# Where a half's products are split: moving the split of the previous block pair in front of the gate's convolution

## The chip, the cores and the metric

The kernel runs on one core of a Trainium2 chip. The metric is the device time of one execution in microseconds (us). Engines are named as in the profile: PE (TensorE matmuls), PEld (its weight loads), DVE (VectorE), ACT (ScalarE), POOL (GpSimd), SP (SyncE, which issues the weight DMAs).

## The reference

The program is a two-layer encoder on 256 positions of width 2048. Layer 0 mixes tokens with grouped-query attention, layer 1 with dilated sliding-window attention; each layer ends with a gated MLP, which the change is about. Cut to that:

```python
def conv_ffn(h, w_up, conv_w, conv_b, w_down):
    u = h @ w_up                                   # 2048 -> 2 * 5632
    u = depthwise_conv(u, conv_w) + conv_b         # width 3 along positions
    gate, val = jnp.split(u, 2, axis=-1)
    return (jax.nn.silu(gate) * val) @ w_down      # 5632 -> 2048
# h = h + conv_ffn(rms_norm(h, ffn_norm[i]), ...), for i in 0, 1
```

## The kernel before

**Products of three.** All is float32. A matmul operand is split into a high part rounded to the fast format (`wh`, `xh`, by ACT) and a low part, the rest (`wl`, by DVE); a product is three matmuls, of high with high, low with high and high with low. So every weight tile of 128 x 1024 costs one ACT rounding (L144, in a fast unit L179) and one DVE subtraction (L145, L180) before TensorE may use it. There are four buffers each of `wh` and `wl`, so DVE can be four tiles ahead of TensorE at most.

**The up-projection** (`ffn`, L492 on) runs in 11 pairs of column blocks of 512: pair p has gate block p and value block 11 + p. The pairs are worked in two halves, 0 to 5 and 6 to 10, and after each half the down-projection consumes its products. A usual block is four calls of `feed`, one for each 512 rows of weights, of 24 matmuls each. Pairs 2, 4, 6 and 8 (`UP`) go through `up_pair`: three feeds for the gate and three for the value, with a "fast unit" in between that does one quarter of both blocks with seven products in place of eight (a Strassen-Winograd step). The unit costs DVE four sums of weights (L178) and seven splits (L180), and a "fold" behind it (L695 to L704) brings its seven results together in a tile with the tag `st`.

**After a gate or value block** its accumulators are evacuated to `stg` by ACT (`evac_scaled`, L489), turned with positions along the free axis by two DVE transposes (L377) and 16 small copies into `u` (`turned`, L562, by POOL; at the end of a half every second one by ACT, L564), convolved by `conv` (4 ACT instructions L541, 8 on DVE, L549) into `cg` for a gate and `cv` for a value. The gate gets its silu (L588). Then `product` multiplies `cg` into `cv` (L578), and `act_split` splits the product into the operands of the down-projection. For blocks 1 and 2 of a half that is `combined`: four subtractions into a tile with the tag `st` (L617), then roundings on ACT (L320) and rests on DVE (L321); for the others it is plain, four roundings (L606) and four rests (L607). `cg`, `cv` and `st` have one buffer each.

**What sets the order.** This work is written as generators that are advanced in small steps between the matmuls. `feed` gives four steps: two advance the list `beside`, two the first generator of the queue `pending`. `up_pair`'s fast unit gives none. `gate_gen(p)` evacuates and turns gate p, waits some steps and then does value p - 1's convolution and product; in an `UP` pair it runs in `beside`, else it queues in `pending`; when `pending` is empty, in layer 0 the generator in `spare` (the bias lines of the next mixer, four small matmuls and a DMA issued by POOL) gets the step. `value_gen(p)` evacuates and turns value p, waits (4 steps after an `UP` pair, 2 after another, 5 after pair 0), does gate p's convolution, its silu, and at last `act_split` of pair p - 1. `flush` does the last value of a half. The generators yield between parts:

```python
for _ in range(4 if gate[0] in UP else 2 if last else 5):
    yield
yield from conv(gate)
yield
nc.scalar.activation(gate[2], gate[2], AF.Silu)
```

The order on each engine is then chosen by a planner, which issues what is ready in its own estimate, the earliest written first; weight splits are treated as if written 60 instructions earlier. An instruction marked `keep_in_program_order` is issued behind all that was written before it on its engine: the convolution's ACT instructions, the roundings of both splits, and the rests of `combined`. Each engine works through its queue strictly in order.

**Sums for the fast units.** `sums` (L651) prepares the operands of `up_pair`: it adds the parts of the normalised input (L655, into `cg`), makes four differences (L663, into `cv`) and splits them (L320, L321). For half 0 it runs beside pair 0, for half 1 in the first steps of pair 6. In the first half the down-projection calls `pair` twice, for output blocks 0, 1 and 2, 3; each call has two fast units of its own, whose sums use the tiles `u`.

Of the kernel before, what the change touches and what calls it, by code (L numbers as in the profile page):

```python
# [8 lines left out]
F32 = mybir.dt.float32  # L9
F32R = mybir.dt.float32r  # L10
AF = mybir.ActivationFunctionType
# [3 lines left out]
P = 128  # L15
D = 2048
NT = 256
NKT = D // P
EPS = 1e-6
NPAIR = 11  # L20
NROW = 32 * NPAIR
HALVES = ((0, 6), (6, 11))
# [3 lines left out]
UP = 2, 4, 6, 8  # L26
# [7 lines left out]
def tile_encoder(ctx: ExitStack, tc: tile.TileContext, x, xT, w_a, w_ao, q_gain, k_gain, w_b, w_bo,  # L34
                 rel_bias, gains, w_up, conv, w_down, final_norm, rope, ident_c, onehot, out):
    nc = tc.nc
# [23 lines left out]
    def nm(s):  # L60
        uid[0] += 1
        return f"{s}_{uid[0]}"
# [15 lines left out]
    def start(gen):  # L78
        if next(gen, StopIteration) is not StopIteration:
            pending.append(gen)  # L80
# [238 lines left out]
    def split_in_order(hi, lo, src):  # L319
        tc.keep_in_program_order(nc.scalar.activation(hi, src, AF.Copy))  # L320
        tc.keep_in_program_order(nc.vector.tensor_tensor(lo, src, hi.bitcast(F32), ALU.subtract))  # L321
# [32 lines left out]
    def pair_slot(kt, shape, dt=F32, name="pr"):  # L354
        return hpool.tile(shape, dt, tag=f"a{kt // 2}", name=nm(name))
# [136 lines left out]
    def ffn(l, hT, ss_in, cw, g_next, last, side=None):  # L492
        with tc.tile_pool(name=nm("fpool"), bufs=1) as fp:
# [41 lines left out]
            def halves(v):  # L535
                return v.rearrange("p (m t) -> p m t", m=2)

            def conv(blk):
                n, u, c = blk
                for j in range(4):  # L540
                    tc.keep_in_program_order(nc.scalar.activation(  # L541
                        halves(c[:, j]), u[:, j, :, :P], AF.Identity, bias=tap(n, j, 3), scale=tap(n, j, 1)))
                    if j == 1:
                        yield
                flat = u.rearrange("p j m t -> p j (m t)")
                for j in range(4):
                    cj = halves(c[:, j])
                    for i, o in ((0, 0), (2, 1)):
                        nc.vector.scalar_tensor_tensor(cj, halves(flat[:, j, o:o + NT])[:, ::-1], tap(n, j, i), cj,  # L549
                                                       ALU.mult, ALU.add)  # L550
                    if j == 1:
                        yield

            def turned(s, u, by_act=False):
                quad = quad_tile(fp, "quad", 2)
                for m in range(2):
                    quad_T(quad, slice(m, 8, 2), s[:, m])
                for i, (q, c) in enumerate(QC):
                    o = u[32 * c:32 * c + 32, :, :, 32 * q:32 * q + 32]
                    src = quad[32 * q:32 * q + 32, c].rearrange("p (j m) t -> p j m t", m=2)  # L560
                    if i % 2 == 0 or not by_act:
                        nc.gpsimd.tensor_copy(o, src)  # L562
                    else:
                        nc.scalar.activation(o, src, AF.Copy)  # L564

            def gate_gen(accs, blk, value):
                s = evac_scaled(fp, accs, rstd, 1)
                yield
                turned(s, blk[1])
                if value is not None:  # L570
                    for _ in range(4 if blk[0] in UP else 2 if blk[0] == 1 else 1):
                        yield
                    yield from product(value)
# [6 lines left out]
            def value_gen(accs, blk, gate, last):  # L580
                s = evac_scaled(fp, accs, rstd, 1)
                yield
                turned(s, blk[1], blk[0] - NPAIR in (HALVES[0][1] - 1, NPAIR - 1))
                for _ in range(4 if gate[0] in UP else 2 if last else 5):
                    yield
                yield from conv(gate)
                yield
                nc.scalar.activation(gate[2], gate[2], AF.Silu)  # L588
                if last is not None:
                    yield  # L590
                    yield from act_split(last)

            def act_split(value):
                slots, k0 = value[4:]
                cv = value[2]
                if k0 // 4 in fast:
                    slots[-1 - k0 // 4], *parts = combined(cv, k0)
                    if hf == 1:
                        plain_too(k0, 20 + 2 * fast.index(k0 // 4), *parts)
                    ready.add(k0 // 4)  # L600
                    yield
                    return
                slots.update(new_slots(range(k0, k0 + 4)))
                for j in range(4):
                    hi, lo = slots[k0 + j]
                    tc.keep_in_program_order(nc.scalar.activation(hi, cv[:, j, :], AF.Copy))  # L606
                    nc.vector.tensor_tensor(lo, cv[:, j, :], hi.bitcast(F32), ALU.subtract)  # L607
                    if j == 1:
                        yield
                ready.add(k0 // 4)  # L610
# [38 lines left out]
            picks = {}  # L649

            def sums(kg, at, r, st):  # L651
                hts = [hT[4 * kg + j][:2] for j in range(4)]
                for j, (hi, lo) in enumerate(hts):
                    with tc.issue_after(newest[0].ins):
                        nc.vector.tensor_tensor(r[:, j], hi.bitcast(F32), lo.bitcast(F32), ALU.add)  # L655
                    if j == 1:
                        yield
                v = r.rearrange("p (b j) (m t) -> p b j m t", b=2, m=2)
                st = st.rearrange("p i (j t) -> p i j t", j=2)
                a11, a21, a12, a22 = v[:, 0, :, 0], v[:, 0, :, 1], v[:, 1, :, 0], v[:, 1, :, 1]  # L660
                yield
                for o, x, y in ((0, a21, a22), (2, a21, a11), (1, a11, st[:, 0]), (3, a12, st[:, 1])):
                    nc.vector.tensor_tensor(st[:, o], x, y, ALU.subtract)  # L663
                yield
                own = [pair_slot(at + 2 * i, [P, 4, 2, P], F32R, "s") for i in range(2)]
                split_in_order(*own, st)
                pick = {q: tuple(tuple(hts[b + j][i][:, m * P:(m + 1) * P] for j in range(2)) for i in range(2))
                        for q, b, m in ((1, 0, 0), (2, 2, 0), (4, 2, 1))}
                for q, i in ((5, 0), (6, 1), (7, 2), (3, 3)):
                    pick[q] = own[0][:, i], own[1][:, i]  # L670
                picks[kg] = pick
# [37 lines left out]
            for hf, (p0, p1) in enumerate(HALVES):  # L709
# [5 lines left out]
                for p in range(p0, p1):  # L715
                    k0 = 4 * (p - p0)
                    cg = fp.tile([P, 4, NT], F32, tag="cg", name=nm("cg"))
                    cv = fp.tile([P, 4, NT], F32, tag="cv", name=nm("cv"))
                    gate, value = (p, next_u(), cg), (NPAIR + p, next_u(), cv, cg, slots, k0)

                    def gate_done(accs, gate=gate, last_value=last_value):
                        gen = gate_gen(accs, gate, last_value)
                        if gate[0] in UP:
                            next(gen)
                            beside.append(gen)
                        else:
                            start(gen)

                    first = partial(sums, 0, 16, cg, cv)
                    if p == p0 and hf == 1:  # L730
                        start(first())
                    if p == 0:
                        va = project2(w_up[l], 0, NPAIR, hT, kgs, 1, gate_done, None, (), [first])
                    elif p in UP:
                        va = up_pair(p, UP_ORDER, gate_done)
                    else:
                        gate_done(project(w_up[l], p, hT, kgs))
                        va = project(w_up[l], NPAIR + p, hT, kgs)
                    extra[0] = fp, ["raw2"]
                    start(value_gen(va, value, gate, last_value))  # L740
                    last_value = value
                    if p == 1 and side is not None:
                        spare.append(side())
# [83 lines left out]
                f0, f1 = ([(kg, None)] for kg in fast)  # L827
                if hf == 0:
                    for ns in (0, 1), (2, 3):
                        pair(wd, ns, slots, both[0] + both[3] + [(4, 0)] + f0 + [(4, 1), (5, 0)] + f1 + [(5, 1)], spot, folds,  # L830
                             None, 3 * (ns[0] == 0), ready)
                    continue
# [596 lines left out]

    hT, ss, cw = mixer_a()  # L1430
    hT, ss = ffn(0, hT, ss, cw, 2, False, bias_lines)
    hT, ss, cw = mixer_b(hT, ss)
    ffn(1, hT, ss, cw, None, True)


# [82 lines left out]
```

## Time and profile before

| | us |
|---|---|
| median of 3 runs | 2240.97 (2240.86 to 2243.26) |
| the profiled execution | 2243.49 |
| its span | 2241.7 |
| PE busy in it | 2219.9 |
| DVE busy | 1879.4 |
| ACT busy | 1344.0 |
| POOL busy | 763.5 |

Times in the trace are us from the start of the span. A matmul is listed with a duration of about 0.39 us, but the next one starts before it ends, so PE looks busy all the time; where TensorE waits a little is seen better in the number of matmuls that start in a stretch. In layer 0 the pairs of the first half run from about 257 to 518, the down-projection from 518 to 649, the second half from 649; in layer 1 the first half ends at about 1781 and the second begins at about 1911.

### The profile page before, as it was taken

The numbers are of one execution on the slowest core, as the hardware profiler recorded it, in microseconds if no ns is written. First come the engines' busy times: TensorE is split into PE (matmuls) and PEld (weight loads), VectorE is DVE, ScalarE is ACT, GpSimd is POOL, SyncE is SP. The second block draws the span as 40 slices with busy tenths as digits, with TensorE's granted clock in tenths as the row PEclk, the third lists the DMA queues.
The fourth block names the chain that finished last, engine by engine and source line by source line (L and its number), as shares of the span: only waits on it lengthen the run. The fifth ranks groups of instructions, "written<-read, shape, count | busy, mean of one in ns | idle before, by whom it ended". The sixth has DMA issues, their size and how long they took to land.

```text
span 2241.7 us, 28897 instructions
## 1 busy us (share of the span) xinstructions
PE 2219.9 (99%) x9957; PEld 1835.3 (82%) x9957; DVE 1879.4 (84%) x2385; ACT 1344.0 (60%) x1894; POOL 763.5 (34%) x1017
## 2 busy tenths in 40 slices
PE   9999999999999999999999999999999999999998
PEld 7888888887888878888888888888888878888887
DVE  6877678998898998968886878588899998989887
ACT  7676656566455666665454556566565755556664
POOL 2343255843006462040053006003746500264611
PEclk9999999999999999999999999999999999999999
DMA  8565655555656555565556555556556555556654
GB/s 302 192 216 187 217 190 190 185 198 179 206 177 226 187 198 196 199 188 195 186 185 201 175 195 171 201 184 216 179 197 213 173 190 204 208 168 208 223 198 141
DMA packets 126180, 439.59 MB, mean 196 GB/s; under 512 B 14408, under 2 KB 18248, under 8 KB 126032
## 3 DMA queue, kind: packets, MB, share of 16 engines
q1 hardware_dynamic: 123056, 429.05, 56.9%
q0 software_dynamic: 2688, 8.39, 1.5%
q8 instruction: 78, 1.28, 0.2%
q14 instruction: 70, 0.57, 0.1%
q10 hardware_dynamic: 288, 0.30, 0.0%
HBM read 432.34 MB, written 5.34 MB: 195 GB/s over the span
## 4 chain that ended last, share of the span: by engine, by line
PE 43%; DVE 9%; issue 2%; POOL 1%; DMA 1%; ACT 1%; DVEq 0%; POOLq 0%; ACTq 0%
PE acc L133 13%; PE acc L134 12%; PE acc L132 12%; DVE wl L145 3%; DVE wl L180 1%; DVE cv L549 1%; PE ps L187 1%; PE ps L188 1%; PE ps L186 1%; POOL u L562 1%; PE acc L187 1%; PE acc L188 1%; DVE cg L549 1%; PE acc L186 1%; DMA raw<-in_w_b_dram 0%
## 5 line engine op out<-in xcount | busy, mean ns | idle before, releaser
L145 DVE TENSOR_TENSOR wl<-raw,wh 128x1024 fp32r<-128x1024 f32 (+1 forms) x716 | 899.1, 1264 | 226.9 <-ACT wh L144 221.1
L144 ACT ACTIVATE wh<-raw 128x1024 fp32r<-128x1024 f32 (+1 forms) x716 | 746.1, 1048 | 519.2 <-PE acc L134 407.0
L133 PE MATMUL acc<-wl,xh 128*128 128x512 f32 x2048 | 799.3, 390 | 4.2 <-DVE wl L145 4.1
L132 PE MATMUL acc<-wh,xh 128*128 128x512 f32 x2048 | 799.1, 390 | 0.3 <-ACT wh L144 0.3
L134 PE MATMUL acc<-wh,xh 128*128 128x512 f32 x2048 | 797.1, 389 | 0.0
L562 POOL COPY u<-quad 32x256 f32<-32x256 f32 x672 | 518.5, 772 | 444.2 <-DVE quad L377 394.9
L133 PEld LDWEIGHTS acc<-wl,xh 128*128 128x128 f32 x2048 | 384.7, 188 | 88.2 <-DVE wl L145 10.1
L132 PEld LDWEIGHTS acc<-wh,xh 128*128 128x128 f32 x2048 | 384.7, 188 | 79.9 <-ACT wh L144 0.7
L134 PEld LDWEIGHTS acc<-wh,xh 128*128 128x128 f32 x2048 | 384.6, 188 | 79.4
L133 PE MATMUL acc<-wl,a 128*128 128x512 f32 x720 | 280.7, 390 | 1.1 <-DVE wl L145 0.9
L132 PE MATMUL acc<-wh,a 128*128 128x512 f32 x720 | 280.9, 390 | 0.0
L134 PE MATMUL acc<-wh,a 128*128 128x512 f32 x720 | 280.1, 389 | 0.0
L179 ACT ACTIVATE wh<-raw 128x1024 fp32r<-128x1024 f32 x112 | 118.3, 1060 | 106.5 <-PE acc L134 76.4
L133 PEld LDWEIGHTS acc<-wl,a 128*128 128x128 f32 x720 | 135.2, 188 | 30.0 <-DVE wl L145 2.8
L134 PEld LDWEIGHTS acc<-wh,a 128*128 128x128 f32 x720 | 135.1, 188 | 28.2 <-DVE a L328 0.2
L132 PEld LDWEIGHTS acc<-wh,a 128*128 128x128 f32 x720 | 135.2, 188 | 27.8
L381 POOL COPY wide<-quad 32x256 f32<-32x256 f32 x133 | 89.8, 675 | 169.3 <-DVE quad L377 159.8
L180 DVE TENSOR_TENSOR wl<-raw,wh 128x1024 fp32r<-128x1024 f32 x112 | 135.6, 1228 | 5.8 <-ACT wh L179 4.4
L398 POOL COPY wide<-quad 32x256 f32<-32x256 f32 x88 | 53.3, 605 | 234.8 <-DVE quad L377 167.8
L489 ACT ACTIVATE stg<-acc,rstd 128x512 f32<-128x512 f32 x122 | 81.2, 681 | 21.4 <-PE acc L134 13.3
L549 DVE SCALAR_TENSOR_TENSOR cg<-u,cw,cg 128x256 f32<-128x256 f32 x176 | 90.8, 560 | 1.9 <-ACT cg L541 1.9
L549 DVE SCALAR_TENSOR_TENSOR cv<-u,cw,cv 128x256 f32<-128x256 f32 x176 | 86.9, 540 | 0.0
(309 smaller groups left out, 2202.4 us busy)
## 6 DMA issues: line engine op xcount, KB each, us to landing
raw<-in_w_up_dram SPq DMA_DIRECT2D x352, 512.0 KB, 4.6
raw<-in_w_down_dram SPq DMA_DIRECT2D x176, 512.0 KB, 4.5
raw<-in_w_b_dram SPq DMA_DIRECT2D x144, 512.0 KB, 4.1
raw<-in_w_bo_dram SPq DMA_DIRECT2D x48, 512.0 KB, 4.0
raw<-in_w_a_dram SPq DMA_DIRECT2D x40, 512.0 KB, 4.8
raw<-in_w_ao_dram SPq DMA_DIRECT2D x32, 512.0 KB, 4.7
raw<-in_w_a_dram SPq DMA_DIRECT2D x16, 256.0 KB, 5.7
there<-quad POOLq DMA_DIRECT2D x6, 512.0 KB, 4.3
```

The lines of the kernel that those rows point to most:

```text
L132: nc.tensor.matmul(accs[m], xh, wh[:, j, :], start=st, stop=False)
L133: nc.tensor.matmul(accs[m], xh, wl[:, j, :], start=False, stop=False)
L134: nc.tensor.matmul(accs[m], xl, wh[:, j, :], start=False, stop=sp)
L144: nc.scalar.activation(wh[:, c], r[:, c], AF.Copy)
L145: newest[0] = nc.vector.tensor_tensor(wl[:, c], r[:, c], wh[:, c].bitcast(F32), ALU.subtract)
L179: nc.scalar.activation(wh, r, AF.Copy)
L180: nc.vector.tensor_tensor(wl, r, wh.bitcast(F32), ALU.subtract)
L381: nc.gpsimd.tensor_copy(o[32 * c:32 * c + 32, :, 32 * q:32 * q + 32], quad[32 * q:32 * q + 32, c])
L398: nc.gpsimd.tensor_copy(dst, src)
L489: nc.scalar.activation(o[:, m, :], accs[m], AF.Copy, scale=rstd[:, m:m + 1])
L549: nc.vector.scalar_tensor_tensor(cj, halves(flat[:, j, o:o + NT])[:, ::-1], tap(n, j, i), cj, ALU.mult, ALU.add)
L562: nc.gpsimd.tensor_copy(o, src)
```

## The change

In `value_gen`, except at the end of a half, the split of the previous pair's product now comes one step after the value is turned, in front of the gate's convolution; the steps that it takes are deducted from the waiting steps, with at least one wait left. The gate's silu is no longer there: it is written in the next pair's `gate_gen`, behind the turning of that gate and in front of the value's convolution and product. At the end of a half (gates 5 and 10) the order is convolution, silu, split, as before, with one waiting step ahead of the convolution in place of two and no step between the convolution and the silu. Third, `sums` is cut in two: `sums_begun` (additions and differences) is started for half 1 in the second call of the down-projection of half 0, after four waiting steps, in tiles of its own with the tags `cg` and `cv`; `sums_made` (the split) is written at the start of pair 6.

```diff
@@ gate_gen
                 turned(s, blk[1])
                 if value is not None:
+                    nc.scalar.activation(value[3], value[3], AF.Silu)
                     for _ in range(4 if blk[0] in UP else 2 if blk[0] == 1 else 1):
                         yield
                     yield from product(value)
@@ value_gen
-                turned(s, blk[1], blk[0] - NPAIR in (HALVES[0][1] - 1, NPAIR - 1))
-                for _ in range(4 if gate[0] in UP else 2 if last else 5):
+                if gate[0] + 1 in (p for _, p in HALVES):
+                    turned(s, blk[1], True)
+                    yield
+                    yield from conv(gate)
+                    nc.scalar.activation(gate[2], gate[2], AF.Silu)
+                    yield
+                    yield from act_split(last)
+                    return
+                turned(s, blk[1])
+                wait = 4 if gate[0] in UP else 5 if last is None else 2
+                if last is not None:
+                    yield
+                    for _ in act_split(last):
+                        yield
+                        wait -= 1
+                    wait -= 1
+                for _ in range(max(wait, 1)):
                     yield
                 yield from conv(gate)
-                yield
-                nc.scalar.activation(gate[2], gate[2], AF.Silu)
-                if last is not None:
-                    yield
-                    yield from act_split(last)
@@ sums
             def sums(kg, at, r, st):
+                yield from sums_begun(kg, r, st)
+                sums_made(kg, at, st)
+
+            def sums_begun(kg, r, st, wait=0):
+                for _ in range(wait):
+                    yield
                 hts = [hT[4 * kg + j][:2] for j in range(4)]
...
                     nc.vector.tensor_tensor(st[:, o], x, y, ALU.subtract)
                 yield
+
+            def sums_made(kg, at, st):
+                hts = [hT[4 * kg + j][:2] for j in range(4)]
                 own = [pair_slot(at + 2 * i, [P, 4, 2, P], F32R, "s") for i in range(2)]
-                split_in_order(*own, st)
+                split_in_order(*own, st.rearrange("p i (j t) -> p i j t", j=2))
@@ the loop over pairs
                     if p == p0 and hf == 1:
-                        start(first())
+                        sums_made(0, 16, early[1])
@@ the down-projection of half 0
                     for ns in (0, 1), (2, 3):
+                        if ns[0] == 2:
+                            early = [fp.tile([P, 4, NT], F32, tag=t, name=nm(t)) for t in ("cg", "cv")]
+                            start(sums_begun(0, *early, 4))
                         pair(wd, ns, slots, both[0] + both[3] + [(4, 0)] + f0 + [(4, 1), (5, 0)] + f1 + [(5, 1)], spot, folds,
                              None, 3 * (ns[0] == 0), ready)
```

## The prediction

> **What bounds the kernel now.** I read the shares of the engines first, then the windows (busy time and count of instructions in equal stretches), then the stretch with the longest loss, in order of time. The columns of a window are its bounds and length, then busy us and (x) instructions for PE, PEld, DVE, ACT and POOL, the granted clock, the DMA share and GB/s.
>
> ```profile
> PE 2219.9 (99%) x9957; PEld 1835.3 (82%) x9957; DVE 1879.4 (84%) x2385; ACT 1344.0 (60%) x1894; POOL 763.5 (34%) x1017
> 480.00:520.00 40.00, 40.00 (x178) 33.14 (x177) 39.06 (x54) 25.44 (x40) 25.61 (x32) 1.00 0.53 183
> 520.00:560.00 40.00, 37.03 (x153) 29.14 (x152) 34.31 (x45) 27.32 (x41) 4.24 (x8) 0.96 0.52 172
> 1742.00:1782.00 40.00, 40.00 (x179) 33.10 (x177) 39.06 (x53) 25.44 (x38) 25.61 (x32) 1.00 0.55 180
> 1782.00:1822.00 40.00, 37.40 (x154) 29.47 (x153) 34.75 (x47) 27.83 (x42) 4.23 (x8) 0.96 0.51 176
> 400.00:420.00 20.00, 20.00 (x90) 16.49 (x89) 19.96 (x29) 14.28 (x19) 14.27 (x20) 1.00 0.53 176
> 420.00:440.00 20.00, 19.34 (x86) 15.67 (x85) 18.60 (x22) 10.71 (x14) 15.46 (x19) 1.00 0.64 220
> 660.00:680.00 20.00, 19.65 (x86) 15.67 (x85) 19.97 (x20) 12.07 (x13) 0.00 (x0) 1.00 0.41 131
> 800.00:820.00 20.00, 19.29 (x83) 14.88 (x82) 19.97 (x27) 12.38 (x16) 12.47 (x16) 1.00 0.50 175
> 1676.00:1696.00 20.00, 19.82 (x88) 16.05 (x87) 18.56 (x23) 13.14 (x18) 13.92 (x16) 1.00 0.65 221
> 1926.00:1946.00 20.00, 19.95 (x88) 15.92 (x87) 19.71 (x22) 12.22 (x14) 0.00 (x0) 1.00 0.52 184
> 2065.00:2085.00 20.00, 19.80 (x87) 15.81 (x86) 19.96 (x26) 12.95 (x18) 12.47 (x16) 1.00 0.57 192
> ```
>
> TensorE is the bound, and no matmul is added or removed. A window in which nothing stops it holds 178 matmuls in 40 us, so one takes 40/178 = 0.2247 us. What can be won is the matmuls missing from other windows. At the end of the first half 178 - 153 = 25 are missing, or 5.6 us, in each of the two layers (179 - 154 again gives 25): 11.2 us. In windows of 20 us with 90 due, pair 3 (420) misses 4, the start of pair 6 (660) 4 and pair 9 (800) 7; layer 1 misses 2, 2 and 3 at the same places. That is 22, or 4.9 us. Everything this change can win is therefore near 16 us, 0.7%; it can lose more.
>
> Now the end of the half. Lines are start, duration, engine, operation, and in brackets the idle time before it with its releaser; those of ACT come first, then POOL's and DVE's; the last three are groups of the window 474 to 484, with busy us and mean ns.
>
> ```profile
> 479.07 1.06 ACT L320 ACTIVATE s<-st 128x1024 fp32r<-128x1024 f32 x1 [0.27 <-DVE st L617]
> ...
> 482.93 2.08 ACT L541 ACTIVATE cv<-u,cw 128x256 f32<-128x256 f32 x4 [1.02 <-DVE sx L321]
> ...
> 491.62 2.08 ACT L541 ACTIVATE cg<-u,cw 128x256 f32<-128x256 f32 x4 [1.99 <-DVE cv L578]
> ...
> 499.17 1.06 ACT L588 ACTIVATE cg<-cg 128x1024 f32<-128x1024 f32 x1 [2.34 <-DVE cg L549]
> 500.14 1.25 ACT L489 ACTIVATE stg<-acc,rstd 128x512 f32<-128x512 f32 x2
> ...
> 517.88 2.08 ACT L541 ACTIVATE cg<-u,cw 128x256 f32<-128x256 f32 x4 [3.76 <-POOL u L562]
> 519.87 1.05 ACT L144 ACTIVATE wh<-raw 128x1024 fp32r<-128x1024 f32 x1
> ...
> 502.96 14.89 POOL L562 COPY u<-quad 32x256 f32<-32x256 f32 x16 [6.87 <-DVE quad L377]
> ...
> 470.63 1.26 DVE L145 TENSOR_TENSOR wl<-raw,wh 128x1024 fp32r<-128x1024 f32 x1 [1.44 <-ACT wh L144]
> ...
> 475.14 0.69 DVE L704 TENSOR_TENSOR acc<-acc,fold 128x512 f32<-128x512 f32 x1
> 475.86 0.96 DVE L617 TENSOR_TENSOR st<-cv 128x256 f32<-128x256 f32 x2
> ...
> L617 DVE TENSOR_TENSOR st<-cv,st 128x256 f32<-128x256 f32 x2 | 1.0, 512 | 0.0
> L321 DVE TENSOR_TENSOR s<-st,s 128x1024 fp32r<-128x1024 f32 x1 | 1.2, 1208 | 0.0
> L321 DVE TENSOR_TENSOR sx<-cv,sx 128x512 fp32r<-128x512 f32 (+1 forms) x2 | 1.0, 544 | 0.0
> ```
>
> Read it as one chain. The split of pair 2's product begins at 475.86, right behind the last addition of pair 4's fold (L704): both use the one buffer `st`. The convolution of value 3 waits for that split (it writes `cv`, which the split reads), the convolution of gate 4 waits for product 3 (L578; it writes `cg`), the silu for that convolution, and the evacuation of gate 5 stands behind the silu at 500.14. So POOL gets gate 5 only at 502.96 and ends at 517.85, and ACT, whose convolution of gate 5 is queued by then, stands 3.76 us with the next rounding of weights (519.87) behind it. TensorE's lead over its split weights is gone from there on, while DVE had been idle before 470.63.
>
> **The change part by part.**
>
> *Split in front of the gate's convolution, pair 4.* Nothing is added; four subtractions and the roundings (1.0 + 1.0 + 1.2 + 1.0 = 4.2 us of DVE, by the rows above) move from 476 into pair 4's first three feeds, some 430 to 440, before the fold takes `st`. Value 3's convolution no longer waits for the fold, so product 3, gate 4's convolution and its silu all come earlier, and the evacuation of gate 5 loses the 2.34 us and the 1.06 us of silu ahead of it: 3.4 us. With POOL's 14.89 us unchanged, gate 5's convolution then begins at 517.88 - 3.4 = 514.5; more than the idle 3.76 us ACT cannot win. The end of the half loses 5.6 us, of which a part is clock:
>
> ```profile
> 549.80:553.20 3.40, 1.52 (x7) 0.97 (x6) 3.37 (x4) 1.06 (x1) 0.00 (x0) 1.00 0.25 82
> 553.20:556.60 3.40, 3.40 (x10) 2.63 (x9) 3.40 (x4) 1.06 (x1) 0.00 (x0) 0.50 0.79 249
> 556.60:560.00 3.40, 3.40 (x16) 2.77 (x16) 2.21 (x3) 2.46 (x3) 0.00 (x0) 1.00 0.38 147
> ```
>
> After the stretch with 7 matmuls the clock is 0.50 for 3.4 us, in which 10 run in place of 16: 6 x 0.2247 = 1.3 us. The pure wait is 5.6 - 1.3 = 4.3 us. Taking 3.4 us out leaves 0.9 us of wait and, as the stretch is then nearly full, no slow clock: I take 4.7 us per layer, 9.4 us; ends 0 (gate 5 comes no earlier) and 11.2. The Trainium skill, "TensorE: Matmul & The Clock Gate", section "What's actually happening", gives a window of 3413 ns and half rate after an idle one; the length agrees with the 3.4 us here, but the stretch before still held 7 matmuls, so a fully idle window isn't needed. By the page's rule no stall under 3.4 us would cost clock, and the rival below would be 1.3 us cheaper per place.
>
> *What it costs at pair 4.* The fast unit that follows draws on the lead:
>
> ```profile
> 431.19 1.23 DVE L145 TENSOR_TENSOR wl<-raw,wh 128x1024 fp32r<-128x1024 f32 x1 [1.37 <-ACT wh L144]
> 442.21 1.23 DVE L180 TENSOR_TENSOR wl<-raw,wh 128x1024 fp32r<-128x1024 f32 x1 [0.74 <-ACT wh L179]
> L180 DVE TENSOR_TENSOR wl<-raw,wh 128x1024 fp32r<-128x1024 f32 x7 | 8.5, 1244 | 0.9 <-ACT wh L179 0.7
> L178 DVE TENSOR_TENSOR raw<-raw,raw 128x1024 f32<-128x1024 f32 x4 | 5.2, 1302 | 0.1
> 451.39 4.62 DVE L180 TENSOR_TENSOR wl<-raw,wh 128x1024 fp32r<-128x1024 f32 x4
> 453.24 0.39 PE L187 MATMUL ps<-wl,s 128*128 128x512 f32 x1
> L607 DVE TENSOR_TENSOR a<-cv,a 128x256 fp32r<-128x256 f32 x4 | 2.3, 612 | 0.0
> ```
>
> The unit needs 8.5 + 5.2 = 13.7 us of DVE for 42 matmuls, 9.4 us. Its tightest weights end at about 451.39 + 1.2 = 452.6 and are used at 453.24: 0.6 us spare, plus idle 1.37 and 0.74 us before, together 2.7 us. Moving 4.2 us in there leaves a stall of 1.5 us. Above: the gate's convolution also steps back by one step (12 matmuls, 2.7 us), which gives 4.2 us, and the slow clock 1.3 more, 5.5. Below: 0, if the lead has room for the rest. I take 1.5, since the idle rows stand right there: 3.0 us in two layers.
>
> *Pairs 2 and 8.* Their splits are plain (2.3 us, L607) and move into DVE time with full lead, but the gate's convolution steps back by 2.7 us; their units hold the same instructions as pair 4's, so 0.6 + 0.74 us are free and the stall is between 0 and 1.4 us. I take 0.7 at four places, the middle, as neither end has a nearer row: 2.8 us.
>
> *Pairs 3 and 9.* The 2.3 us of plain splits leave the work just ahead of them. The losses there are 4, 7, 2 and 3 matmuls, 0.9, 1.6, 0.4 and 0.7 us, all under 2.3: 3.6 us won; end 0 if the queue only reorders.
>
> *Sums for pair 6.* Their additions and subtractions move into the down-projection's second call:
>
> ```profile
> L655 DVE TENSOR_TENSOR cg<-xh 128x256 f32<-128x256 f32 x4 | 1.7, 414 | 0.0
> L663 DVE TENSOR_TENSOR cv<-cg 128x256 f32<-128x256 f32 x2 | 0.8, 416 | 0.0
> L663 DVE TENSOR_TENSOR cv<-cg,cv 128x256 f32<-128x256 f32 x2 | 0.8, 416 | 0.0
> L145 DVE TENSOR_TENSOR wl<-raw,wh 128x1024 fp32r<-128x1024 f32 x5 | 6.1, 1224 | 4.6 <-ACT wh L144 4.5
> ```
>
> These groups, 3.3 us in all, leave the window 640 to 680; the last row is the group of 590 to 606, where DVE idles 4.6 us waiting for ACT and the sums can hide (without that cover they cost their 3.3 us). The loss at pair 6 is 4 and 2 matmuls, 1.3 us: won; end 0.
>
> *Silu in front of the product, halves' ends.* The silu (1.06 us) is the same instruction, ready when its convolution ends; ACT is 60% busy, and I price it at nothing; it would cost its 1.06 us at ACT's head if a rounding waited behind. At the halves' ends the convolution, silu and split only come one or two steps sooner, behind the same POOL copies: nothing. SP's queue is as before. On POOL's, the small DMA of the bias lines in `spare` comes a few steps earlier in pairs 2 and 3, as `pending` empties sooner; only the next mixer waits for it: nothing.
>
> Sum: -9.4 - 3.6 - 1.3 + 3.0 + 2.8 = -8.5 us. The profiled execution took 2243.49 us (span 2241.7); it would be 2235.0. It lies 2.5 us above the median of the runs, 2240.97, and I put the forecast against the median: 2232.5 us, -0.38%.
>
> **The rivals.** *Half's end unrelieved:* gate 5 still reaches POOL at 503, since the queue's order is a planner's and another wait takes the place of the silu. For it: the order is not written out; against: each link of the chain is shown. Then -3.6 - 1.3 + 5.8 = +0.9 us, 2241.9.
>
> *The fast units eat the gain:* all high ends, 2 x 5.5 + 4 x 1.4 = 16.6 us against 14.3 won: +2.3, 2243.3. For it: only 0.6 us spare; against: DVE has 2.1 us idle just ahead.
>
> *Slower: ACT blocked by early splits.* The rounding in the split is queued on ACT in program order; put ahead of the gate's convolution it can reach the head before DVE's subtractions are done, and the weights' roundings stand behind it, as they did for 3.76 us at 517.88. Places: pairs 3, 4, 9 and 10 of both layers, 8. At 3.76 us each it costs 30 us, less 14.3: +15.8, 2256.8; it decides from (14.3 + 4.5)/8 = 2.4 us a place. For it: DVE is full at 400 to 420 (19.96 of 20 us), so its data are late there; against: ACT waited for the split's subtractions only 0.27 us at 479.07.
>
> **How the numbers follow.** About 0.2%, 4.5 us, is what a measurement of this kernel can tell from no change. Forecast 0.71; unrelieved 0.08 and eaten 0.07 (both within 0.2%); blocked 0.14. The likeliest case has its own range 2225 (all 16 us won, no new stall) to 2236. To leave out no more than 2 in 10 the range goes up past the two middle cases, to 2244: 2225 to 2244. Faster 0.71, same 0.15, slower 0.14.
>
> **What would show it.** Right: st<-cv of pair 2 near 425 to 436 and no longer behind L704; gate 5's convolution on ACT near 514 with little idle; 520 to 560 with some 174 matmuls at clock 1.00; 660 to 680 with 90. Wrong: 440 to 460 missing over 10 matmuls or at a lower clock; POOL's copies of gate 5 still ending near 518; ACT idle for some us before L320 or L606.

## The result, and the profile after

The changed kernel takes 2241.70 us (median of 12 runs, 2240.00 to 2244.87); the kernel before, run on the same chip, takes 2243.59 us (2240.86 to 2245.51). The ratio is 0.9994 with a 95% interval of 0.9985 to 1.0003: no difference that can be told. The profiled execution after took 2244.87 us, with a span of 2243.1 (before: 2243.49 and 2241.7).

The forecast was a gain of 8.5 us. That nothing is left of it does not mean that nothing happened. These are windows of the changed kernel's trace, in the same columns as those shown of before (bounds, length, then busy us and instructions of PE, PEld, DVE, ACT and POOL, clock, DMA share, GB/s), behind the line of the engines' shares:

```profile
PE 2218.4 (99%) x9957; PEld 1833.9 (82%) x9957; DVE 1885.2 (84%) x2385; ACT 1344.4 (60%) x1894; POOL 762.8 (34%) x1017
520.00:560.00 40.00, 40.00 (x178) 33.11 (x177) 37.05 (x50) 30.39 (x46) 4.71 (x9) 1.00 0.59 181
1782.00:1822.00 40.00, 39.73 (x176) 32.59 (x175) 37.77 (x49) 30.79 (x46) 4.39 (x8) 1.00 0.55 180
660.00:680.00 20.00, 20.00 (x90) 16.54 (x90) 18.09 (x18) 12.30 (x13) 0.00 (x0) 1.00 0.52 178
400.00:420.00 20.00, 17.32 (x75) 13.82 (x74) 17.96 (x25) 14.24 (x22) 10.75 (x16) 1.00 0.51 158
440.00:460.00 20.00, 19.13 (x85) 15.53 (x84) 19.86 (x22) 11.67 (x14) 13.37 (x16) 1.00 0.35 107
780.00:800.00 20.00, 18.20 (x80) 14.42 (x79) 20.00 (x26) 11.14 (x16) 14.98 (x20) 1.00 0.46 151
1660.00:1680.00 20.00, 19.30 (x85) 15.67 (x84) 19.45 (x29) 11.47 (x17) 11.15 (x16) 1.00 0.57 181
2045.00:2065.00 20.00, 18.16 (x79) 14.73 (x80) 19.76 (x26) 11.25 (x17) 12.64 (x17) 1.00 0.55 167
```

The end of the half is full: 178 and 176 matmuls at clock 1.00, where 153 and 154 stood. So is the start of pair 6 (660 to 680: 90). In exchange, pair 3 lost 15 of the 90 matmuls due in 400 to 420, where before had all 90, and pair 9 lost 10 and 11 (780 to 800 and 2045 to 2065).

To put a price on each place I compared the start of the same-numbered matmul in both traces at the bounds of the pairs (TensorE runs the same 9957 matmuls in both; a few stand in another order inside pairs 2 and 6). The step of that difference, in us, is what each stretch lost (+) or won (-):

| stretch | forecast, both layers | layer 0 | layer 1 |
|---|---|---|---|
| pairs 2 and 8 | +2.8 | -0.33, +0.17 | +0.15, +0.28 |
| pair 3 | in the next row | +2.20 | +1.22 |
| pair 9 (forecast: pairs 3 and 9) | -3.6 | +1.35 | +2.45 |
| pair 4 | +3.0 | +1.17 | +1.49 |
| end of the half | -9.4 | -5.28 | -3.97 (+0.83 later in the down-projection) |
| sums, pair 6 | -1.3 | -0.80 | -0.54 |
| all the rest (mixers) | 0 | +1.64 | -0.66 |

The last row is from the mixers, which the change does not touch. In the first one the changed kernel has a stretch at half clock, but that is not what the 1.6 us are: four kernels of the experiments lose 1.3 to 2.2 us between the same matmuls (140 to 180) without a slow stretch, so it looks like scatter between traces. The sum is +1.4 us, which is the difference of the spans. Without the mixers it is +0.4: everything that was won at the ends of the halves and at pair 6 (9.25 - 0.83 + 1.34 = 9.8 us) was paid out again in pairs 3, 9 and 4 (7.2 + 2.7).

**Where it was won.** The chain at the end of the first half, as far as it shows in ACT's and POOL's timelines and, in the last line, DVE's (the lines of the file have moved: L628 is the L617 of before, L723 and L724 are L703 and L704):

```profile
431.85 1.04 ACT L320 ACTIVATE s<-st 128x1024 fp32r<-128x1024 f32 x1
...
502.14 1.25 ACT L489 ACTIVATE stg<-acc,rstd 128x512 f32<-128x512 f32 x2
...
520.35 2.08 ACT L541 ACTIVATE cg<-u,cw 128x256 f32<-128x256 f32 x4 [1.56 <-POOL u L562]
...
505.62 14.69 POOL L562 COPY u<-quad 32x256 f32<-32x256 f32 x16 [7.69 <-DVE quad L377]
...
427.89 1.15 DVE L628 TENSOR_TENSOR st<-cv,st 128x256 f32<-128x256 f32 x2
```

Pair 2's split now has the last two of its subtractions at 427.89 and its rounding at 431.85, ahead of pair 4's fold. TensorE is 4.67 us later by then, so on the scale of before the evacuation of gate 5 is at 502.14 - 4.67 = 497.5 (before 500.14) and its convolution at 515.7 (before 517.88, forecast 514.5), and ACT waits 1.56 us for POOL instead of 3.76. That is 2.2 us earlier; with the 1.3 us of slow clock that are gone it makes 3.5 of the 5.28 us.

A second thing changed at this place. The edit at the halves' ends, which the prediction priced at nothing, brings the first two roundings of a plain split ahead of the silu of gate 5. ACT of the kernel before comes first, then that of the changed one:

```profile
528.24 1.04 ACT L588 ACTIVATE cg<-cg 128x1024 f32<-128x1024 f32 x1
...
530.14 1.32 ACT L606 ACTIVATE a<-cv 128x256 fp32r<-128x256 f32 x4
```

```profile
523.28 0.71 ACT L617 ACTIVATE a<-cv 128x256 fp32r<-128x256 f32 x2
...
530.71 1.04 ACT L588 ACTIVATE cg<-cg 128x1024 f32<-128x1024 f32 x1
```

Every kernel below whose half's end is full has this edit as well, so its share of the gain was not separated from that of the chain.

**Where it was lost.** Pair 9 of the first layer, first DVE, then the lines of ACT that feed it:

```profile
792.21 1.41 DVE L145 TENSOR_TENSOR wl<-raw,wh 128x1024 fp32r<-128x1024 f32 x1
793.55 1.41 DVE L321 TENSOR_TENSOR s<-st,s 128x1024 fp32r<-128x1024 f32 x1
794.88 1.42 DVE L321 TENSOR_TENSOR sx<-cv,sx 128x512 fp32r<-128x512 f32 x2
796.22 0.61 DVE L321 TENSOR_TENSOR c<-cv,c 128x256 fp32r<-128x256 f32 x1
796.76 1.42 DVE L145 TENSOR_TENSOR wl<-raw,wh 128x1024 fp32r<-128x1024 f32 x1
...
790.71 1.06 ACT L320 ACTIVATE s<-st 128x1024 fp32r<-128x1024 f32 x1 [3.30 <-DVE st L628]
...
792.81 2.94 ACT L144 ACTIVATE wh<-raw 128x1024 fp32r<-128x1024 f32 x3
```

Two things are to be seen here, and they are two theories. ACT stands 3.30 us in front of the split's rounding, and three roundings of weights come behind it in one piece: the prediction's rival of the blocked ACT. And DVE does all four rests of the split in a row between two rests of weights, which begin 796.76 - 792.21 = 4.55 us apart, while TensorE uses one up in 12 matmuls, 2.7 us. TensorE stops at 798 for 1.5 us, until the second of them is done.

In pair 3 of the first layer both come together, with POOL as a third. ACT's lines stand first, then DVE's:

```profile
399.40 1.10 ACT L541 ACTIVATE cg<-u,cw 128x256 f32<-128x256 f32 x2 [4.29 <-POOL u L562]
400.41 1.04 ACT L144 ACTIVATE wh<-raw 128x1024 fp32r<-128x1024 f32 x1
...
403.37 1.06 ACT L320 ACTIVATE s<-st 128x1024 fp32r<-128x1024 f32 x1 [0.94 <-DVE st L628]
...
401.48 1.33 DVE L145 TENSOR_TENSOR wl<-raw,wh 128x1024 fp32r<-128x1024 f32 x1 [1.84 <-ACT wh L144]
402.73 0.61 DVE L628 TENSOR_TENSOR st<-cv,st 128x256 f32<-128x256 f32 x1
403.26 1.68 DVE L549 SCALAR_TENSOR_TENSOR cg<-u,cw,cg 128x256 f32<-128x256 f32 x3
404.87 1.41 DVE L321 TENSOR_TENSOR s<-st,s 128x1024 fp32r<-128x1024 f32 x1
406.21 1.41 DVE L321 TENSOR_TENSOR sx<-cv,sx 128x512 fp32r<-128x512 f32 x2
407.54 2.75 DVE L145 TENSOR_TENSOR wl<-raw,wh 128x1024 fp32r<-128x1024 f32 x2
```

The gate's convolution waits 4.29 us for POOL's copies with a rounding of weights behind it; DVE idles 1.84 us for that rounding and then does 4.8 us of other work in one piece (402.73 to 407.54). TensorE loses 3.1 us at 406 to 409; the step in the table is smaller, since before lost 0.9 us in the same pair.

### The profile page after: what moved, and what is told of

The parts are those of the page before. It is cut to its first block, busy times and chain, and to the rows that moved or that the text cites. A ratio compares the mean times of both kernels' runs of the same rounds, so it can differ in the third digit from the quotient of the medians.

```text
span 2243.1 us, 28885 instructions
## 1 busy us (share of the span) xinstructions
PE 2218.4 (99%) x9957; PEld 1833.9 (82%) x9957; DVE 1885.2 (84%) x2385; ACT 1344.4 (60%) x1894; POOL 762.8 (34%) x1017
## 4 chain that ended last, share of the span: by engine, by line
PE 42%; DVE 8%; issue 2%; DMA 2%; POOL 1%; ACT 1%; DVEq 0%; POOLq 0%; ACTq 0%
PE acc L133 12%; PE acc L132 12%; PE acc L134 12%; DVE wl L145 3%; DVE wl L180 1%; DVE cv L549 1%; PE ps L187 1%; PE ps L188 1%; PE ps L186 1%; DMA raw<-in_w_b_dram 1%; POOL u L562 1%; DMA raw<-in_w_up_dram 1%; ACT wh L144 1%; DMA raw<-in_w_down_dram 1%; DVE cg L549 1%
```

## The experiments

All times are medians on the chip; each ratio is to the kernel before on the same chip, with its 95% interval. The steps by stretch are worked out as in the table above. `FRONT` names the gates whose convolution has the split in front of it (gate 2 is convolved in pair 3, gate 3 in pair 4, gate 8 in pair 9). Where a line is named by its number, the experiments' kernels have it somewhat further down: the subtractions into st are L628 to L637, the split's roundings and rests L320, L321, L640 and L645.

A step comes from one trace of each kernel, and some places scatter. In pair 9 three kernels below keep the old split, with the same instructions in the same order on DVE, ACT and POOL as in the kernel before; their steps are -0.15, -0.20 and -0.87 in the first layer and +1.19, +0.34 and +1.31 in the second. So a step of pair 9 in the second layer says little below 1.3 us.

### One part alone: the split of pair 4

The changed kernel, with the old order for every gate that is not in `FRONT`:

```
+FRONT = (3,)
...
-                    nc.scalar.activation(value[3], value[3], AF.Silu)
+                    if value[0] - NPAIR in FRONT:
+                        nc.scalar.activation(value[3], value[3], AF.Silu)
...
+                if gate[0] not in FRONT:
+                    turned(s, blk[1])
+                    for _ in range(4 if gate[0] in UP else 2 if last else 5):
+                        yield
+                    yield from conv(gate)
+                    yield
+                    nc.scalar.activation(gate[2], gate[2], AF.Silu)
+                    if last is not None:
+                        yield
+                        yield from act_split(last)
+                    return
```

> The kernel before with the split in front of the gate's convolution (and the silu in front of the product) in pair 4 alone; the halves' ends and the sums for pair 6 as in the changed kernel; pairs 1 to 3 and 7 to 10 in the old order. Theory 'blocked' (the roundings of the early splits in pairs 3 and 9 stand on ACT for data of DVE and hold the roundings of the weights back, which gave the gain back): all other steps stay as measured in the changed kernel, half's ends -5.3 and -4.0 (then +0.8), pair 4 +1.2 and +1.5, sums -0.8 and -0.5, and pairs 3 and 9 are those of the kernel before: -7.1 us, ratio 0.9968. Rival 'whole shift' (the half's end is only relieved when every split before it is early too): the half's ends stay as before, pair 4 costs its 2.7 us, sums -1.3: +1.4 us, ratio 1.0006.

Measured: 2235.37 us, ratio 0.9960 (0.9947 to 0.9972). The steps: pair 3 +0.22 and -0.12, pair 4 +1.42 and +1.43, end of the half -5.52 and -5.40, pair 6 -0.80 and -0.54, pair 9 -0.15 and +1.19. Its windows (before had 153 and 154 matmuls in the two ends of the halves):

```profile
516.00:556.00 40.00, 40.00 (x178) 33.11 (x178) 37.44 (x49) 29.84 (x44) 4.41 (x8) 1.00 0.61 185
1774.00:1814.00 40.00, 40.00 (x178) 33.13 (x177) 37.47 (x49) 29.84 (x44) 4.41 (x8) 1.00 0.58 187
400.00:420.00 20.00, 20.00 (x90) 16.48 (x89) 19.97 (x28) 13.87 (x19) 14.33 (x19) 1.00 0.55 176
440.00:460.00 20.00, 18.88 (x83) 15.31 (x83) 19.86 (x20) 12.64 (x13) 10.11 (x12) 1.00 0.36 114
```

The one early split that the half's end needs is pair 4's; the rival that it takes the whole shift falls. Here ACT's convolution of gate 5 begins at 515.18, which is 514.0 on the scale of before (TensorE is 1.17 us later) and near the forecast 514.5. It comes 3.9 us earlier, and with the 1.3 us of clock that is 5.2 of the 5.5 us. This kernel is faster than both, by about what was forecast for the whole change, with less of it.

### The early split in pairs 3 and 9 alone

The kernel before, its sums and halves' ends included, with the split in front for two gates:

```
+FRONT = 2, 8
```

> The kernel before with the early split and its silu in pairs 3 and 9 alone; all else as before. Theory 'blocked': the four places cost what they cost in the changed kernel, 2.2 + 1.35 + 1.2 + 2.45 = +7.2 us, ratio 1.0032, ACT idle 1 to 3.3 us in front of the rounding of st in these pairs, and the half's ends as in the kernel before. Rival 'neighbours' (the loss in pairs 3 and 9 comes from the other edits around them, such as the plain splits that moved from there): under 2 us in all, ratio under 1.001.

Measured: 2248.89 us, ratio 1.0022 (1.0013 to 1.0031): slower, by 5.0 us. The steps: pair 9 +1.25 and +2.21, as in the changed kernel; pair 3 only -0.03 and +0.18, but pair 4 +1.11 and +1.07; end of the half -0.20 and +0.30; pair 6 +0.06 and +0.30. Windows, and ACT's wait in pair 9:

```profile
520.00:560.00 40.00, 37.25 (x153) 29.35 (x152) 34.15 (x47) 27.89 (x43) 4.70 (x9) 0.96 0.57 186
796.00:806.00 10.00, 8.91 (x40) 7.06 (x39) 10.00 (x14) 4.78 (x8) 6.72 (x9) 1.00 0.45 138
...
794.65 1.06 ACT L321 ACTIVATE s<-st 128x1024 fp32r<-128x1024 f32 x1 [2.30 <-DVE st L631]
```

The half's end is untouched (153 matmuls, slow clock), so these splits have no part in the gain. Pair 9's loss in the first layer is theirs alone; in the second layer up to 1.3 of the 2.2 us also stand in kernels with the old split there. Pair 3's loss is not theirs alone: by itself the early split there costs nothing in the pair and 1.1 us in the next. And as the sums and the halves' ends stay old here, pair 6 wins nothing; this agrees with the sums being what wins there elsewhere.

### The old order in pairs 3 and 9 alone

The changed kernel with the code of the first experiment and this set:

```
+FRONT = 1, 3, 4, 6, 7, 9
```

> The changed kernel with the old order (convolution, silu, split) in pairs 3 and 9 alone. Theory 'blocked': the 7.2 us of these places go and the rest stays: 6.5 to 7.5 us under the changed kernel, ratio to the kernel before 0.9965 to 0.997. Rival 'moved on' (a late split in pair 3 keeps st and ACT busy into pair 4, whose early split then comes late): the stall of pair 4 grows from 1.2 to 3 us or more, and half's ends lose part of their gain; ratio 0.9985 or above.

Measured: 2235.75 us, ratio 0.9964 (0.9952 to 0.9977). Steps: pair 3 +0.83 and +0.36, pair 9 -0.19 and +0.62, pair 4 +1.43 and +1.39, end of the half -5.48 and -5.25. Taking the four places out gives back 5.6 of their 7.2 us, and nothing moves on to pair 4: this is where most of the gain had gone.

### Where in those pairs: ACT's wait, or DVE's order

First only the subtractions stay in front, and the roundings and rests go behind the convolution, in pairs 3 and 9 (`rest` first yields behind the subtractions):

```
+                if gate[0] in (2, 8):
+                    yield
+                    rest = act_split(last, 1)
+                    for _ in (next(rest), 1, 2):
+                        yield
+                    yield from conv(gate)
+                    yield
+                    yield from rest
+                    return
...
```

> The changed kernel, but in pairs 3 and 9 only the four subtractions of the split stay in front of the gate's convolution; its roundings (ACT) and the rests (DVE) are issued behind the convolution, so that on ACT one or two roundings of weights more come ahead of the first of them. Theory 'blocked': no wait of over 1 us in front of that rounding, and the loss of the four places falls from 7.2 to under 2.5 us: about 5 us under the changed kernel. Rival 'load' (the 1.9 us of subtractions in a stretch in which DVE is full are what is late): the places lose as in the changed kernel, 6 us or more, and the time stays within 1.5 us of it.

Measured: 2239.56 us, ratio 0.9982 (0.9973 to 0.9991). The four places lose, in order of time, 1.22, 0.11, 1.85 and 1.27, in all 4.45 us instead of 7.22. ACT's wait in front of the rounding is 1.02 us in pair 9, and DVE's rests stand apart:

```profile
788.43 1.07 ACT L320 ACTIVATE s<-st 128x1024 fp32r<-128x1024 f32 x1 [1.02 <-DVE st L637]
...
794.75 1.41 DVE L321 TENSOR_TENSOR s<-st,s 128x1024 fp32r<-128x1024 f32 x1
796.09 0.68 DVE L321 TENSOR_TENSOR sx<-cv,sx 128x512 fp32r<-128x512 f32 x1
796.69 1.21 DVE L145 TENSOR_TENSOR wl<-raw,wh 128x1024 fp32r<-128x1024 f32 x1
```

About 40% of the loss goes, less than either theory asked for in full, and the edit removed ACT's wait and the piece on DVE together. So the next kernel touches DVE's order and leaves ACT's wait. The roundings are issued at once, as in the changed kernel, and the second and third rest two steps later, behind the newest rest of weights (`apart` is 0, 2, 0):

```
-                split_in_order(*own, st)
-                split_in_order(hA, lA, v[:, :, :, 0])
-                split_in_order(hB, lB, a22)
+                todo = (*own, st), (hA, lA, v[:, :, :, 0]), (hB, lB, a22)
+                if apart:
+                    for hi, lo, src in todo:
+                        tc.keep_in_program_order(nc.scalar.activation(hi, src, AF.Copy))
+                    for n, (hi, lo, src) in zip(apart, todo):
+                        for _ in range(n):
+                            yield
+                        with tc.issue_after(newest[0].ins):
+                            tc.keep_in_program_order(nc.vector.tensor_tensor(lo, src, hi.bitcast(F32), ALU.subtract))
...
```

> The changed kernel, but in pair 9 of both layers and pair 3 of the second the last rests of the early split (L321: sx 128x256, and in pair 9 c 128x256) stand on DVE behind the next rest of weights instead of ahead of it; ACT's queue is the same but for the rounding of c, which comes some places earlier; pair 3 of the first layer is untouched. The one place's rounding of st still waits 3.3 us on ACT with the weights' roundings behind it. New theory 'bunched rests' (ACT's wait costs nothing by itself; the weights' rest is late because DVE, in order and full, does up to 3.4 us of the split's rests in one piece, between 793.55 and 796.76, more than the 2.7 us in which TensorE uses one up): the stalls at 798 and 2061 (1.6 us each by start times of the matmuls) fall to 0.4 us or less, that at 1671 (1.0) to 0.5; 2.5 to 3 us under the changed kernel. Rival 'blocked' (ACT's wait sets the time): both stalls keep at least 1.1 us, total within 1 us of the changed kernel.

Measured: 2242.27 us, ratio 0.9994 (0.9985 to 1.0002): no faster than the changed kernel. But at the place itself, pair 9 of the first layer, the window, then ACT, then DVE:

```profile
780.00:800.00 20.00, 20.00 (x90) 16.54 (x89) 20.00 (x26) 11.27 (x16) 15.22 (x20) 1.00 0.53 166
...
790.96 1.06 ACT L640 ACTIVATE s<-st 128x1024 fp32r<-128x1024 f32 x1 [2.99 <-DVE st L633]
...
795.13 0.88 DVE L645 TENSOR_TENSOR sx<-cv,sx 128x512 fp32r<-128x512 f32 x1
795.93 1.42 DVE L145 TENSOR_TENSOR wl<-raw,wh 128x1024 fp32r<-128x1024 f32 x1
797.27 0.61 DVE L645 TENSOR_TENSOR sx<-cv,sx 128x256 fp32r<-128x256 f32 x1
```

ACT still waits 2.99 us, and the stop at 798 is gone: 90 matmuls instead of 80. Not all of that is the edit. This trace comes into the pair with its weights further ahead: the rest at 792.46 lies 14.57 us behind the pair's first matmul, that at 792.21 in the changed kernel 15.95. So the smaller stop at 783, which lies ahead of the edited instructions, is gone too. The second layer shows the edit more plainly: there ACT still waits 3.00 us (3.31 in the changed kernel), and the stop at 2059 falls from 1.45 to 0.37 us, by about the two rests (0.6 us each) that now stand behind the weights' rest. So in pair 9 ACT's wait was not what TensorE stood for; DVE's order was. DVE's windows agree: with 20.00 of 20 us busy at 780 to 800 in both kernels it never stood idle for a rounding there. The steps: pair 9 -0.08 and +1.87 (were +1.35 and +2.45), pair 3 of the second layer +1.69 (was +1.22). Part of what is won is lost again 8 to 12 us later in the same pair (stops of 0.3 and 0.7 us at 801 and 809): DVE is busy 20.00 of 20 us, and the rests that were put off have to be done all the same. The three places that were touched won 1.5 us, not 2.5 to 3. The untouched one, pair 3 of the first layer, lost 1.9 us more in this profile, most of it by a slow clock, which is shown at the end.

### What pair 3 needs beside its own split

Early splits in pairs 3 and 4 alone, the sums and the halves' ends as in the changed kernel:

```
+FRONT = 2, 3
```

> The kernel before with the early split (and its silu) in pairs 3 and 4 alone; the halves' ends and the sums as in the changed kernel. Theory 'two splits in one pair' (the early split of pair 4 begins its subtractions inside pair 3; with pair 3's own split early too, DVE has 48.6 us of work there in place of 46.5, and the lead runs out, while either split alone costs pair 3 under 0.3 us): pair 3 loses 2.2 and 1.2 us as in the changed kernel, all else as in the kernel with pair 4's split alone, so about 3.5 us over it: ratio 0.9975. Rival 'the plain splits' (pair 3's loss needs those of pairs 2 and 8, moved in the changed kernel): pair 3 loses under 0.5 us, ratio 0.996.

Measured: 2236.68 us, ratio 0.9971 (0.9960 to 0.9982). Pair 3 loses +0.33 and +0.88, and its window 400 to 420 holds 86 matmuls, with DVE full:

```profile
400.00:420.00 20.00, 19.64 (x86) 15.65 (x85) 20.00 (x30) 14.09 (x20) 12.01 (x18) 1.00 0.56 179
```

Two early splits in one pair are thus not enough for the 2.2 us of the first layer: that theory falls there, and accounts for most of the 1.2 us of the second. With pair 2's early split alone beside pair 4's (the kernel with the old order in pairs 3 and 9) the pair lost 0.83 and 0.36. None of the sets with two of these three splits that were run gives the loss of the first layer, which all three together do; pairs 2 and 3 without 4 were not run, and which of the waits shown above (ACT for POOL, DVE's long piece) carries the rest was not separated.

### Pair 4: rests behind the fast unit

The kernel with pair 4's split alone, whose pieces in sx are rounded behind the fast unit (`rest` first yields behind the subtractions and the rounding and rest of st):

```
+                if gate[0] == 3:
+                    yield
+                    rest = act_split(last, True)
+                    next(rest)
+                    yield
+                    yield
+                    yield from conv(gate)
+                    for _ in range(4):
+                        yield
+                    yield from rest
+                    return
```

> The kernel with the early split in pair 4 alone, and there the roundings and rests of the pieces in sx (1.1 us of DVE) are issued behind the fast unit instead of ahead of it; the subtractions and the rest of st stay in front. Theory (pair 4's stall of 1.4 us is the unit's lead over DVE, eaten by the split's 4.2 us): the stall falls by 1.1 to about 0.3 us in each layer, and as product 3 comes some us later but still ahead of the silu of gate 4 by what the half's end needs, that end keeps its gain: about 2 us under the kernel with the early split in pair 4 alone, ratio 0.995. Rival (product 3 is on the chain of the half's end): a stall of 1 us or more comes back between 520 and 560, and nothing is won.

Measured: 2235.92 us, ratio 0.9961 (0.9947 to 0.9974). Pair 4's step falls from 1.42 and 1.43 to 0.53 and 0.53, and the end of the half is full, though its step is 0.5 us less (-4.96 and -4.94):

```profile
440.00:460.00 20.00, 19.80 (x87) 16.04 (x87) 19.86 (x20) 12.52 (x13) 9.90 (x11) 1.00 0.40 115
520.00:560.00 40.00, 40.00 (x178) 33.11 (x177) 36.60 (x45) 29.04 (x41) 4.40 (x8) 1.00 0.60 190
```

The stop of the unit is the lead that the split ate, as the prediction had it: 87 matmuls instead of 83 with 1.1 us of DVE work moved away. What is left, 0.9 us in each layer less 0.5 at the halves' ends, is below what the times resolve: the two kernels cannot be told apart.

One part of the change is no change in what runs. With the silu written right behind the gate's convolution again, the scheduler that orders the queues puts every engine's instructions in the same order as in the changed kernel.

## Why the prediction was right and wrong

That 2241.70 us lies within the forecast range, 2225 to 2244, is luck: the likeliest case ended at 2236, and the range went up from there to take in two rivals, neither of which is what happened. The terms of the sum, one by one:

*Half's end, 4.7 us per layer:* right in size, 5.28 and 3.97 (5.5 and 5.4 with pair 4's split alone), and the chain moved as told: split ahead of the fold, silu and evacuation earlier, full windows, no slow clock. The kernel with that one split shows that no other early split is needed. How much of the gain is the chain's stays open, as the new order at the halves' ends, priced at nothing, comes with it in every kernel that has the gain. The rival of the unrelieved end falls.

*Sums for pair 6, 1.3 us:* right, 0.80 + 0.54.

*Pair 4, 1.5 us per layer:* right in size (1.17 and 1.49) and, by the rests moved behind the unit, in mechanism. It is not the only way to lose there, though: with pair 3's split early and pair 4's late the same unit lost 1.1, and why was not settled.

*Pairs 2 and 8, 0.7 us at four places:* over-priced; +0.3 us in all. The middle between two bounds was not what the rows called for: the plain splits found room.

*Pairs 3 and 9, 3.6 us won:* this is the step that failed. It let "the 2.3 us of plain splits leave the work just ahead of them" and took all the losses of these pairs as won. It left out what comes in from behind: in the order of the change, each of these pairs also gets its own combined split (4.2 us of DVE and three roundings or more) some 6 us earlier, and pair 3 the subtractions of pair 4's too. The prediction counted that for pair 4 alone, where the fold made it look for it. The four places lost 7.2 us, 10.8 off (of the 7.2 up to 1.3, in pair 9 of the second layer, may be scatter); the rest of the sum was off by 2 us.

*The rival of the blocked ACT* had named these pairs, with 2.4 us a place as the point from which the change loses. The wait was there (0.9 to 3.3 us in front of the rounding of st), the loss 1.2 to 2.5 us at four of its eight places; pair 10 lost nothing, and pair 4 is told above. But its mechanism is only partly right. In pair 9 the wait itself cost nothing that shows, as the stop shrank by the rests that were moved while 3.0 us of wait stayed; what cost was the order on DVE, in which 3.2 us of rests stand in one piece ahead of the weights' next rest (793.55 to 796.76). The Trainium skill, "PSUM — Partial Sum Buffer", section "Engine vs sequencer instructions", calls the queues of ScalarE, VectorE and GpSimdE strict FIFO; the trace agrees on ACT, which stood 3.30 us with three roundings of weights behind the one that waited. In pair 9 it is DVE's queue, not ACT's, in which the order was decisive. Against the rival the prediction had put that ACT waited only 0.27 us at 479.07 in the old order. That row is from a place where DVE had been idle 1.44 us some 8 us before; in a pair where DVE is full it says nothing.

*The rival of the fast units* is not what happened: pair 4 took 2.7 us, not 11.

One reading was 1% off: a window's count includes matmuls that run into it, so a matmul takes 0.2267 us from start to start in a full stretch, not 0.2247; no term changes by more than 0.1 us.

## What to carry to other kernels

When work is moved forward as one change in many places, price every place by itself: what leaves it, and also what arrives from the next one. Where an engine is full (DVE 19.96 of 20 us in the window), the question is not how much work is there but how long a piece stands between two deliveries to the bound engine, against the 2.7 us that one delivery lasts and the lead that is left. And try the one place that the chain asks for before the general rule: pair 4 alone gave 0.4%, the whole change nothing.

## What was not expected of the hardware

The same stop of TensorE can cost a stretch at half clock or not. The stop of pair 3 stands in the changed kernel at 406 to 409 and, with the same instructions, in the kernel with the rests apart at 407 to 410. Windows of 3.41 us, laid so that the records' slow stretches (which begin at 144.64 and 410.70) are on their bounds; first the changed kernel, where the later two windows lie 76 such lengths further on, then the other:

```profile
141.23:144.64 3.41, 1.45 (x8) 1.09 (x7) 3.41 (x6) 1.83 (x3) 1.72 (x1) 1.00 0.73 205
144.64:148.05 3.41, 3.41 (x11) 2.83 (x11) 2.22 (x4) 0.99 (x3) 0.00 (x0) 0.50 0.58 143
404.05:407.47 3.42, 2.28 (x9) 1.31 (x7) 3.42 (x5) 3.42 (x6) 3.13 (x6) 1.00 0.44 144
407.47:410.88 3.41, 1.87 (x8) 1.57 (x9) 3.41 (x5) 1.58 (x2) 3.23 (x4) 1.00 0.19 53
```

```profile
403.87:407.28 3.41, 2.98 (x13) 1.99 (x11) 3.41 (x6) 2.72 (x4) 3.12 (x6) 1.00 0.44 153
407.28:410.70 3.42, 1.01 (x3) 0.65 (x4) 3.42 (x5) 2.96 (x4) 3.19 (x5) 1.00 0.00 1
410.70:414.11 3.41, 3.41 (x9) 2.65 (x9) 3.41 (x6) 0.00 (x0) 2.01 (x3) 0.50 0.78 249
```

Where the stop lies across a bound, the two windows are busy 2.28 and 1.87 us and the clock stays; where it lies within one window, that is busy 1.01 us and the next runs at half clock, with 9 matmuls in place of 15. In the mixer a window busy 1.45 us (and at the half's end of before one of 1.52) was followed by half clock too. The windows keep their beat through a whole trace: the slow stretches of one trace begin a whole number of 3.4133 us apart (553.22, 1816.15 and 2239.40 in the kernel before, 370 and 494 lengths; 144.64 and 2240.42 in the changed one, 614). The Trainium skill, "TensorE: Matmul & The Clock Gate", section "What's actually happening", says that the window runs freely; these traces agree. It names an idle window as the condition, and here a window busy for 1.0 to 1.5 of 3.41 us was enough. As the beat lies otherwise against the kernel's work in each trace, a stop of 2 to 3 us costs the time of 15 - 9 = 6 matmuls, some 1.3 us, more or not, by chance. That is most of the 1.9 us that pair 3 lost in one profile more than in the other.
